# Scores of a token with itself and with its block-of-two neighbour: products by element, summed with a matrix of ones

## The chip, the core and the metric

The kernel runs on one core of a Trainium2 chip. A core has a matrix engine (PE, TensorE), a vector engine (DVE, VectorE), a scalar engine (ACT, ScalarE), GpSimd (POOL) and a queue engine (SP) that issues DMAs. Each engine works through its own list of instructions in order and waits on semaphores for the others. PE writes its results into PSUM; the other operands lie in SBUF, 128 partitions wide. The metric is device time in microseconds of one execution, lower being better; the median of three runs is given.

## The reference, cut to what matters

One encoder layer on 256 tokens of 2048 channels: a bidirectional HGRN2 mixer (gated linear recurrence, 16 heads of 128 channels, both directions summed), an output projection, a gated feed-forward net with a short convolution, RMS norms around each. The part that the change touches is the recurrence, which the kernel computes as a matrix of scores per head:

```python
def step(S, inp):
    qi, ki, gi, vi = inp
    b = jnp.cumsum(gi, axis=2)
    inter = jnp.einsum('nhtk,nhkv->nhtv', qi * jnp.exp(b), S)
    diff = b[:, :, :, None, :] - b[:, :, None, :, :]
    decay = jnp.exp(jnp.where(causal_in_chunk, diff, -jnp.inf))
    scores = jnp.einsum('nhtk,nhsk,nhtsk->nhts', qi, ki, decay)
    intra = jnp.einsum('nhts,nhsv->nhtv', scores, vi)
    ...
```

With forget gates f (one set for each direction) and k = 1 - f, the score of token t with an earlier token s is the sum over the 128 channels of q(t) k(s) times all gates from s+1 to t; the backward direction mirrors it. A token's score with itself is the sum of q(t) (k_forward(t) + k_backward(t)).

## The kernel before, in words

**Matrix products.** All weights are fp32. For each `sub` (256 rows by 512 columns of a weight matrix) ACT rounds the raw tile to fp32r (`whi`, L129) and DVE takes the remainder (`wlo = raw - whi`, L130). The activations are split the same way, and PE multiplies hi by hi, hi by lo and lo by hi. `gemm` (L140, matmuls at L174, L177 and L178, 12 of 512 columns per sub) gives tokens on partitions; `gemm_t` (L185, L206 with 512 columns and L209 with 256, 8 of each per sub) gives channels on partitions. `prep` runs LOOK = 3 subs ahead of PE, and `whi` and `wlo` have 4 buffers each, so ACT may write a buffer once PE has finished with the sub four places earlier.

**Scores.** The 16 heads are handled in four groups of HG = 4. For a group, q, the gates f and k = 1 - f of both directions lie with channels on partitions: `qT`, `f`, `ks` and `qs` (tiles of 128 x 1024 per direction; `qs` is q times the gate). The scores of a head with 256 tokens are two 128 x 128 diagonal blocks (`Sd`, eight per group) and two blocks across the halves (`So`). `Sd` is put together by doubling. `diag` (L407) adds the two directions of k into `kc` (L410), multiplies kc and q on PE (L415, eight fp32 matmuls of 128 columns in two calls) and keeps the diagonal with a product by the identity (L416). `level(lev)` (L426) for lev = 0 to 6 fills the pairs whose tokens lie in the two halves of a block of 2m tokens, m = 2^lev: eight fp32 matmuls of 128 columns (L435) of `kc` with `halves(qs, m)`, which takes each block's first m columns from one direction and its other m from the other direction, 1024 + m elements away; then `ks` and `qs` are multiplied by gates for the next level (L439, L442), the gates by each other (`bp`, L446), and the scores are copied into `Sd` where a mask says so (L454). `gather` (L422, on ACT) copies the same interleaving of `ks` into `kc`, which has one buffer. `across` (L456) makes `So`.

**What sets the order.** These closures are put into the queue `later` (two diag, seven levels, two across), and `gemm` and `gemm_t` take one closure from `soon` or `later` after each sub (`step`, L102), so the scores' work is strewn among the next projections' matmuls. The build then lists the instructions of each engine in an order of its own, by a simulated timeline, so that the order on an engine isn't that of the code. The score matmuls use PSUM tiles with the tag `tp`, which has two buffers. `nat` is a pool whose tags have two buffers (`qn` holds gate and sigmoid intermediates); tags of `hp` have one unless it says otherwise (`kc`, `bp0`).

Of the kernel before, what the change touches and what calls it, by code (L numbers as in the profile page):

```python
# [11 lines left out]
F32 = mybir.dt.float32  # L12
F32R = mybir.dt.float32r
U8 = mybir.dt.uint8
AF = mybir.ActivationFunctionType
ALU = mybir.AluOpType
AX = mybir.AxisListType

P = 128
T = 256  # L20
# [3 lines left out]
HG = 4  # L24
# [22 lines left out]
def encoder_layer(  # L47
# [12 lines left out]
    nc = tc.nc  # L60
    V, S, G = nc.vector, nc.scalar, nc.gpsimd

    def pool(stack, name, bufs=1, **kw):
        return stack.enter_context(tc.tile_pool(name=name, bufs=bufs, **kw))
# [14 lines left out]
    ident = const.tile([P, P], F32, name="ident")  # L79
# [20 lines left out]
    soon, later, extra = deque(), deque(), []  # L100
# [229 lines left out]
    rstack = ExitStack()  # L330
    hp = pool(rstack, "hgrn")
    nat = pool(rstack, "nat", 2)
    nsub_h = 2 * HG

    def silu_nat(ps, m, dst):
# [48 lines left out]
    def cut(t, off, dims):  # L384
        return bass.AP(t.tensor, t.offset + off, [list(t.ap[0])] + dims)

    def halves(t, m, c0=0, n=HG * T):


        return cut(t, c0, [[2 * m, n // (2 * m)], [HG * T + m, 2], [1, m]])  # L390

    def do_scores(g):

        q, ks, qs = st["q", g], st["k", g], st["d", g]  # L400
        Sd = hp.tile([P, nsub_h, P], F32, name="Sd", tag="Sd", bufs=2)
        So = [hp.tile([P, HG, P], F32, name="So", tag=f"So{d}", bufs=2) for d in range(2)]
        st["S", g] = (Sd, So)
        bp = [st["f", g]]
        kc = [None]

        def diag(i):  # L407
            if i == 0:
                kc[0] = hp.tile([P, HG, T], F32, name="kc", tag="kc")
                V.tensor_tensor(kc[0], ks[:, 0], ks[:, 1], op=ALU.add)  # L410
            sc = ps_t.tile([P, HG, P], F32, name="sc", tag="tp")
            for j in range(HG):
                h, b = (HG * i + j) // 2, (HG * i + j) % 2
                sl = slice(b * P, (b + 1) * P)
                nc.tensor.matmul(sc[:, j, :], kc[0][:, h, sl], q[:, h, sl], start=True, stop=True)  # L415
            V.tensor_tensor(  # L416
                Sd[:, HG * i : HG * i + HG, :], sc, ident[:, None, :].broadcast_to([P, HG, P]), op=ALU.mult
            )
            if i == 1:
                gather(1)  # L420

        def gather(m):  # L422
            kc[0] = hp.tile([P, HG, T], F32, name="kc", tag="kc")
            S.copy(kc[0].rearrange("p h (n two m) -> p (h n) two m", two=2, m=m), halves(ks, m))  # L424

        def level(lev):  # L426
            m = 1 << lev
            scs = []
            for i in range(2):
                sc = ps_t.tile([P, HG, P], F32, name="sc", tag="tp")  # L430
                for j in range(HG):
                    h, b = (HG * i + j) // 2, (HG * i + j) % 2
                    sl = slice(b * P, (b + 1) * P)
                    r = halves(qs, m, h * T + b * P, P)
                    nc.tensor.matmul(sc[:, j, :], kc[0][:, h, sl], r, start=True, stop=True)  # L435
                scs.append(sc)
            w = HG * T // m
            act = lambda t: cut(t, 0, [[HG * T + m, 2], [2 * m, w // 2], [1, m]])
            V.tensor_tensor(act(ks), act(ks), cut(bp[0], 1, [[w - 1, 2], [2, w // 2], [0, m]]), op=ALU.mult)  # L439
            if lev < NLEV - 1:  # L440
                gather(2 * m)
            V.tensor_tensor(act(qs), act(qs), cut(bp[0], w + 1, [[-(w + 1), 2], [2, w // 2], [0, m]]), op=ALU.mult)  # L442
            if lev < NLEV - 1:
                nbp = hp.tile([P, 2, w // 2], F32, name="bp", tag=f"bp{lev}")
                bv = cut(bp[0], 0, [[2, w], [1, 2]])
                V.tensor_tensor(nbp.rearrange("p d n -> p (d n)"), bv[:, :, 0], bv[:, :, 1], op=ALU.mult)  # L446
                bp[0] = nbp
            for i, sc in enumerate(scs):
                sd = Sd[:, HG * i : HG * i + HG, :]
                if lev == NLEV - 1:  # L450
                    S.copy(sd[:m, :, m:], sc[:m, :, m:])
                    S.copy(sd[m:, :, :m], sc[m:, :, :m])
                else:
                    V.copy_predicated(sd, mk[:, lev, None, :].broadcast_to([P, HG, P]), sc)  # L454

        def across(d):  # L456
            sc = ps_t.tile([P, HG, P], F32, name="sc", tag="tp")
            s0, t0 = d * P, (1 - d) * P
            for h in range(HG):
                nc.tensor.matmul(  # L460
                    sc[:, h, :], ks[:, d, h, s0 : s0 + P], qs[:, 1 - d, h, t0 : t0 + P], start=True, stop=True
                )
            S.copy(So[d], sc)

        later.extend([lambda: diag(0), lambda: diag(1)])
        later.extend([lambda lev=lev: level(lev) for lev in range(NLEV)])
        later.extend([lambda: across(0), lambda: across(1)])

# [48 lines left out]
    for part, g in ORDER:  # L517
        if part == "q":
            do_q(g)
        elif part == "f":  # L520
            do_f(g, 0)
        elif part == "b":
            do_f(g, 1)
            do_scores(g)
        elif part == "g":
            do_g(g)
        else:
            do_v(g)
            do_o(g)
# [221 lines left out]
```

## Time and profile before

| what | value |
|---|---|
| median of 3 runs | 1376.47 us (1376.24 to 1377.78) |
| the profiled execution, its own time | 1377.04 us |
| its span (first to last instruction) | 1375.3 us |
| granted TensorE clock, mean | 0.998 |
| ACT busy | 695.0 us (51%) |
| POOL busy | 13.5 us (1%) |
| HBM traffic | 248.93 MB, mean 181 GB/s |

Busy time of an engine is the time in which at least one of its instructions runs. PE's matmuls overlap in the profile: a row's mean duration covers the pipeline, and the rate has to be taken from how far apart their starts lie. A 128-column fp32 matmul of the program appears as two PE instructions (eight of them as x16). The times in the views of the trace count from the span's start. The scores of the four groups are made from about 90 to 157, 222 to 289, 355 to 422 and 461 to 552 us.

### The profile page before, as it was taken

The page shows a single profiled execution, that of the slowest core. Times are in us where ns is not written, and L with a number is a line of the kernel's source. Part 1 is how long each engine was busy: PE and PEld are TensorE (multiplying, and loading weights), DVE is VectorE, ACT ScalarE, POOL GpSimd, SP SyncE. Part 2 cuts the span into 40 slices and gives each one's busy share as a digit, 9 for nine tenths or more (in the row PEclk, how much of TensorE's full clock was granted, in tenths as well). Part 3 has the DMA queues.
Part 4 walks back from the last instruction along what each step waited for, and adds up shares of the span by engine and source line. Part 5 has one row for each costly group of instructions (what it writes and reads, how often), then busy time and mean ns, then how long its engine had stood idle before and what let it go on. Part 6 is the DMA issues. An engine that isn't in the chain of part 4 may idle for free.

```text
span 1375.3 us, 18411 instructions
## 1 busy us (share of the span) xinstructions
PE 1364.0 (99%) x7362; PEld 1180.4 (86%) x7362; DVE 940.1 (68%) x1188; ACT 695.0 (51%) x971; POOL 13.5 (1%) x21
## 2 busy tenths in 40 slices
PE   9999999999999999999999999999999999999997
PEld 7888988898898888888888888888888888888886
DVE  5687678866886876567668676877677775444444
ACT  5644454454544444456655555555555554434442
POOL 0000000000000000000000000000000000000000
PEclk9999999999999999999999999999999999999999
DMA  7554355435535444663555555555555555555552
GB/s 282 185 187 150 124 186 181 153 124 186 181 123 184 157 149 153 245 235 109 207 184 183 197 181 203 184 184 185 186 198 183 197 184 214 193 204 183 191 205 94
DMA packets 36998, 248.93 MB, mean 181 GB/s; under 512 B 4144, under 2 KB 4912, under 8 KB 7472
## 3 DMA queue, kind: packets, MB, share of 16 engines
q1 hardware_dynamic: 36912, 247.75, 51.2%
q8 instruction: 58, 0.95, 0.3%
q14 instruction: 28, 0.23, 0.0%
HBM read 245.63 MB, written 2.10 MB: 180 GB/s over the span
## 4 chain that ended last, share of the span: by engine, by line
PE 98%; issue 0%; DMA 0%; DVE 0%; SPq 0%; ACT 0%; DVEq 0%; POOLq 0%; POOL 0%
PE pg L206 36%; PE pg L209 18%; PE pg L178 13%; PE pg L177 13%; PE pg L174 13%; PE sc L435 4%; PE sc L491 1%; PE sc L460 1%; PE sc L492 1%; PE sc L415 1%; DMA xs<-in_x 0%; PE tp L233 0%; PE tp L587 0%; PE tp L290 0%; DVE fw L688 0%
## 5 line engine op out<-in xcount | busy, mean ns | idle before, releaser
L130 DVE TENSOR_TENSOR wlo<-raw,whi 128x1024 fp32r<-128x1024 f32 (+1 forms) x457 | 556.6, 1220 | 364.8 <-ACT whi L129 364.4
L129 ACT CAST whi<-raw 128x1024 fp32r<-128x1024 f32 (+1 forms) x457 | 478.3, 1049 | 508.8 <-PE pg L178 226.1
L206 PE MATMUL pg<-hh,whi 128*128 128x512 f32 x1344 | 355.2, 393 | 0.0
L206 PEld LDWEIGHTS pg<-hh,whi 128*128 128x128 f32 x1344 | 234.1, 189 | 34.7
L209 PEld LDWEIGHTS pg<-hh,wlo 128*128 128x128 f32 x1344 | 197.4, 190 | 22.6
L206 PE MATMUL pg<-xx,whi 128*128 128x512 f32 x768 | 208.6, 399 | 0.1
L209 PE MATMUL pg<-hh,wlo 128*128 128x256 f32 x1344 | 203.3, 281 | 0.0
L206 PEld LDWEIGHTS pg<-xx,whi 128*128 128x128 f32 x768 | 134.6, 190 | 20.2 <-DVE xx L298 0.7
L174 PE MATMUL pg<-whi,gg 128*128 128x512 f32 x352 | 136.9, 389 | 0.0
L177 PE MATMUL pg<-wlo,gg 128*128 128x512 f32 x352 | 136.9, 389 | 0.0
L178 PE MATMUL pg<-whi,gg 128*128 128x512 f32 x352 | 136.9, 389 | 0.0
L209 PEld LDWEIGHTS pg<-xx,wlo 128*128 128x128 f32 x768 | 113.0, 191 | 12.4
L209 PE MATMUL pg<-xx,wlo 128*128 128x256 f32 x768 | 117.4, 283 | 0.0
L177 PE MATMUL pg<-wlo,xx 128*128 128x512 f32 x256 | 101.0, 395 | 0.0
L174 PE MATMUL pg<-whi,xx 128*128 128x512 f32 x256 | 100.2, 391 | 0.0
L178 PE MATMUL pg<-whi,xx 128*128 128x512 f32 x256 | 100.0, 390 | 0.0
L177 PEld LDWEIGHTS pg<-wlo,gg 128*128 128x128 f32 x352 | 66.1, 188 | 13.8
L174 PEld LDWEIGHTS pg<-whi,gg 128*128 128x128 f32 x352 | 66.1, 188 | 13.7
L178 PEld LDWEIGHTS pg<-whi,gg 128*128 128x128 f32 x352 | 66.1, 188 | 13.5
L435 PEld LDWEIGHTS sc<-qs,kc 128*128 128x128 f32 x448 | 57.6, 192 | 1.9
L424 ACT COPY kc<-ks 128x1024 f32<-128x1024 f32 x28 | 32.1, 1147 | 52.4 <-PE sc L435 48.5
L435 PE MATMUL sc<-qs,kc 128*128 128x128 f32 x448 | 58.5, 285 | 0.0
(128 smaller groups left out, 1187.3 us busy)
## 6 DMA issues: line engine op xcount, KB each, us to landing
raw<-in_w_up SPq DMA_DIRECT2D x88, 1024.0 KB, 4.9
raw<-in_w_in SPq DMA_DIRECT2D x78, 1024.0 KB, 4.9
raw<-in_w_dn SPq DMA_DIRECT2D x44, 1024.0 KB, 4.9
raw<-in_w_o SPq DMA_DIRECT2D x16, 1024.0 KB, 4.9
x<-in_x SPq DMA_DIRECT2D x1, 2048.0 KB, 7.9
wp<-in_post SPq DMA_DIRECT2D x2, 1024.0 KB, 5.7
out<-fw SPq DMA_DIRECT2D x8, 256.0 KB, 2.6
xs<-in_x SPq DMA_DIRECT2D x3, 512.0 KB, 9.9
```

The source lines that it names most:

```text
L129: S.copy(hi[:, j], src[:, j])
L130: V.tensor_tensor(lo[:, j], src[:, j], hi[:, j].bitcast(F32), op=ALU.subtract)
L174: mm = nc.tensor.matmul(ps[m], a, hi[:, j, :], start=(k == 0), stop=False)
L177: nc.tensor.matmul(ps[m], a, lo[:, j, :], start=False, stop=False)
L178: nc.tensor.matmul(ps[m], b, hi[:, j, :], start=False, stop=(k == 2 * nsub - 1))
L206: nc.tensor.matmul(ps[n], w, xx[:, k], start=(k == 0), stop=False)
L209: nc.tensor.matmul(ps[n][:, 0, :], w, xx[:, k, 0, :], start=False, stop=(k == 2 * nsub - 1))
L415: nc.tensor.matmul(sc[:, j, :], kc[0][:, h, sl], q[:, h, sl], start=True, stop=True)
L424: S.copy(kc[0].rearrange("p h (n two m) -> p (h n) two m", two=2, m=m), halves(ks, m))
L435: nc.tensor.matmul(sc[:, j, :], kc[0][:, h, sl], r, start=True, stop=True)
L460: nc.tensor.matmul(sc[:, h, :], ks[:, d, h, s0 : s0 + P], qs[:, 1 - d, h, t0 : t0 + P], start=True, stop=True)
L491: nc.tensor.matmul(o[:, h, :], Sd[:, 2 * h + b, :], v[:, b, cs], start=True, stop=False)
```

## The change

The self scores and the level-0 scores aren't taken from a full 128 x 128 product any more. The two operands are multiplied element by element on DVE (`products`, a tile `pr` of 128 x 1024), the product is split into an fp32r part `prh` (ACT) and a remainder `prl` (DVE), and PE sums both over the channels by a matmul with a 128 x 128 matrix of ones as weights and 512 columns moving (`sums`). Each row of the result holds the sums of all tokens, of which the identity (self) or the mask of level 0 picks its own. `own` makes the products for the self scores; `diag` sums them, makes the products for level 0 and writes the diagonal; level 0 sums instead of multiplying. The gather into `kc` for level 0 is gone; `prh` lives in the buffer of `kc`, `prl` in that of `bp0`, `pr` in `qn`. The closures in `later` are as many as before.

```diff
+    ones = hp.tile([P, P], F32R, name="ones")
+    S.activation(ones, ident, AF.Copy, scale=0.0, bias=1.0)
...
-        def diag(i):
-            if i == 0:
-                kc[0] = hp.tile([P, HG, T], F32, name="kc", tag="kc")
-                V.tensor_tensor(kc[0], ks[:, 0], ks[:, 1], op=ALU.add)
+        def products(k, r, p=None):
+            if p is None:
+                p = nat.tile([P, HG * T], F32, name="pr", tag="qn")
+            V.tensor_tensor(p.rearrange("p (n j) -> p n j", j=2), k, r, op=ALU.mult)
+            ph = hp.tile([P, HG * T], F32R, name="prh", tag="kc")
+            pl = hp.tile([P, HG * T], F32R, name="prl", tag="bp0")
+            S.copy(ph, p)
+            V.tensor_tensor(pl, p, ph.bitcast(F32), op=ALU.subtract)
+            pr[0] = (ph, pl)
+
+        def sums(i):
             sc = ps_t.tile([P, HG, P], F32, name="sc", tag="tp")
-            for j in range(HG):
-                h, b = (HG * i + j) // 2, (HG * i + j) % 2
-                sl = slice(b * P, (b + 1) * P)
-                nc.tensor.matmul(sc[:, j, :], kc[0][:, h, sl], q[:, h, sl], start=True, stop=True)
-            V.tensor_tensor(
-                Sd[:, HG * i : HG * i + HG, :], sc, ident[:, None, :].broadcast_to([P, HG, P]), op=ALU.mult
-            )
-            if i == 1:
-                gather(1)
+            o = sc.rearrange("p h t -> p (h t)")
+            for j, a in enumerate(pr[0]):
+                nc.tensor.matmul(o, ones, a[:, i * 512 : i * 512 + 512], start=(j == 0), stop=(j == 1))
+            return sc
+
+        def own():
+            p = nat.tile([P, HG * T], F32, name="pr", tag="qn")
+            V.tensor_tensor(p.rearrange("p (h t) -> p h t", t=T), ks[:, 0], ks[:, 1], op=ALU.add)
+            pairs = lambda t: t.rearrange("p (n j) -> p n j", j=2)
+            products(pairs(p), pairs(q.rearrange("p h t -> p (h t)")), p)
+
+        def diag():
+            scs = [sums(i) for i in range(2)]
+            w = HG * T
+            products(cut(ks, w + 1, [[2, w // 2], [-(w + 1), 2]]), cut(qs, 0, [[2, w // 2], [w + 1, 2]]))
+            for i, sc in enumerate(scs):
+                V.tensor_tensor(
+                    Sd[:, HG * i : HG * i + HG, :], sc, ident[:, None, :].broadcast_to([P, HG, P]), op=ALU.mult
+                )
...
             for i in range(2):
+                if lev == 0:
+                    scs.append(sums(i))
+                    continue
                 sc = ps_t.tile([P, HG, P], F32, name="sc", tag="tp")
...
-        later.extend([lambda: diag(0), lambda: diag(1)])
+        later.extend([own, diag])
```

The lines behind the insertions move: in the changed kernel the sum of the two directions is L433, the products L417, the remainder L421, the sums L428, the updates of `ks`, `qs` and `bp` L466, L469 and L473, the diagonal L442, the masked copies L481 and the level matmuls L462.

On DVE, in the first group, from the point where the second direction's `ks` and `qs` are done, the kernel before has:

```order
L446 TENSOR_TENSOR bp<-f 128x1024
L410 TENSOR_TENSOR kc<-ks 128x1024
L130 TENSOR_TENSOR wlo<-raw,whi 128x1024
L446 TENSOR_TENSOR bp<-bp 128x512
L130 TENSOR_TENSOR wlo<-raw,whi 128x1024
L446 TENSOR_TENSOR bp<-bp 128x256
L130 TENSOR_TENSOR wlo<-raw,whi 128x1024
L446 TENSOR_TENSOR bp<-bp 128x128
L446 TENSOR_TENSOR bp<-bp 128x64
L446 TENSOR_TENSOR bp<-bp 128x32
L416 TENSOR_TENSOR Sd<-sc,ident 128x512
```

The changed kernel has at the same place:

```order
L433 TENSOR_TENSOR pr<-ks 128x1024
L130 TENSOR_TENSOR wlo<-raw,whi 128x1024
L417 TENSOR_TENSOR pr<-ks,qs 128x1024
L417 TENSOR_TENSOR pr<-pr,qT 128x1024
L130 TENSOR_TENSOR wlo<-raw,whi 128x1024
L466 TENSOR_TENSOR ks<-ks,f 128x2x512
L469 TENSOR_TENSOR qs<-qs,f 128x2x512
L130 TENSOR_TENSOR wlo<-raw,whi 128x1024
L421 TENSOR_TENSOR prl<-pr,prh 128x1024
L130 TENSOR_TENSOR wlo<-raw,whi 128x1024 x2
L340 SCALAR_TENSOR_TENSOR gg<-pg,rs_137,sg 128x512 x2
L130 TENSOR_TENSOR wlo<-raw,whi 128x1024
```

Both products and the level-0 updates of `ks` and `qs` now stand ahead of the diagonal, with `wlo` operations between them, and the products of gates (`bp`) come after level 0 (its first stands behind the first masked copy).

On PE, the kernel before has the first group's self scores in one piece between the matmuls of a projection:

```order
L177 MATMUL pg<-wlo,xx 128x512
L178 MATMUL pg<-whi,xx 128x512
L174 MATMUL pg<-whi,xx 128x512
L415 MATMUL sc<-qT,kc 128x128 x8
L177 MATMUL pg<-wlo,xx 128x512
```

The changed kernel has, for the level-0 sums of the same group:

```order
L428 MATMUL sc<-prh,ones 128x512
L174 MATMUL pg<-whi,xx 128x512
L177 MATMUL pg<-wlo,xx 128x512
L178 MATMUL pg<-whi,xx 128x512
L174 MATMUL pg<-whi,xx 128x512
L428 MATMUL sc<-prl,ones 128x512
L177 MATMUL pg<-wlo,xx 128x512
L178 MATMUL pg<-whi,xx 128x512
L428 MATMUL sc<-prh,ones 128x512
L428 MATMUL sc<-prl,ones 128x512
```

The sums stand singly among the projection's matmuls. Counting the projections' 512-column matmuls that stand ahead of them in PE's list, the first score matmul of group 0 moves from behind 265 to behind 281, its first level-0 matmul from behind 289 to behind 324, and its level-1 matmuls from behind 320 to behind 353. The remainders of the self scores (`prl`, L428) stand behind 300, the first of level 0 behind 328. In the third group (`ks` and `qs` of which are needed while the fourth group's q and f are projected) `across` moves from behind 680 of the 256-column matmuls to behind 704, the last of that projection.

More of the change, by code (lines that the diff above doesn't have):

```diff
@@ L405, in do_scores @@
         kc = [None]
-        def diag(i):
-            if i == 0:
-                kc[0] = hp.tile([P, HG, T], F32, name="kc", tag="kc")
-                V.tensor_tensor(kc[0], ks[:, 0], ks[:, 1], op=ALU.add)
-            sc = ps_t.tile([P, HG, P], F32, name="sc", tag="tp")
-            for j in range(HG):
-                h, b = (HG * i + j) // 2, (HG * i + j) % 2
-                sl = slice(b * P, (b + 1) * P)
-                nc.tensor.matmul(sc[:, j, :], kc[0][:, h, sl], q[:, h, sl], start=True, stop=True)
-            V.tensor_tensor(
-                Sd[:, HG * i : HG * i + HG, :], sc, ident[:, None, :].broadcast_to([P, HG, P]), op=ALU.mult
-            )
-            if i == 1:
-                gather(1)
+        pr = [None]
+        def products(k, r, p=None):
[8 more added lines that the diff above has]
+        def sums(i):
+            sc = ps_t.tile([P, HG, P], F32, name="sc", tag="tp")
+            o = sc.rearrange("p h t -> p (h t)")
[15 more added lines that the diff above has]
+                )
         def gather(m):
```

## The prediction

> **What bounds the kernel now.** I read the page first: the span, the busy shares and the chain that ended last.
>
> ```profile
> span 1375.3 us, 18411 instructions
> PE 1364.0 (99%) x7362; PEld 1180.4 (86%) x7362; DVE 940.1 (68%) x1188; ACT 695.0 (51%) x971; POOL 13.5 (1%) x21
> PE 98%; issue 0%; DMA 0%; DVE 0%; SPq 0%; ACT 0%; DVEq 0%; POOLq 0%; POOL 0%
> PE pg L206 36%; PE pg L209 18%; PE pg L178 13%; PE pg L177 13%; PE pg L174 13%; PE sc L435 4%; PE sc L491 1%; PE sc L460 1%; PE sc L492 1%; PE sc L415 1%; DMA xs<-in_x 0%; PE tp L233 0%; PE tp L587 0%; PE tp L290 0%; DVE fw L688 0%
> ```
>
> The chain that sets the end is 98% PE, and the two lines that the change rewrites, L415 and L435, lie on it. A busy PE alone would prove little, since matmuls overlap, so the view of waits is asked for PE, and then for what the weights' preparation waits for.
>
> ```profile
> PE tp L290 <- DMA xs<-in_x: 1.6, 1, 1.6
> PE tp L269 <- POOL ident masks.py:199: 1.4, 1, 1.4
> ```
>
> ```profile
> DVE wlo L130 <- ACT whi L129: 364.4, 329, 3.4
> ACT whi L129 <- PE pg L178: 226.1, 148, 2.6
> ACT whi L129 <- PE pg L206: 209.5, 143, 3.1
> ```
>
> PE waits for data twice, both at the start, 3.0 us in all; it never waits for a weight or a score operand. Behind it the order of dependence is the reverse of starvation: DVE waits for ACT, and ACT waits for PE to give a buffer back. So a microsecond less on PE in the scores is a microsecond less of the span, as long as PE's operands still come in time.
>
> **What PE loses and gains.** The chain in order of time has each score step as one piece, start and duration:
>
> ```profile
> 98.69 1.78 PE sc L415 x16
> 105.93 2.66 PE sc L435 x16
> 115.64 1.92 PE sc L435 x16
> 123.25 1.78 PE sc L435 x16
> ...
> 469.11 1.78 PE sc L415 x16
> 476.35 2.66 PE sc L435 x16
> ```
>
> The self scores of a group cost 1.78 us, level 0 costs 2.66, level 1 costs 1.92 and the later ones 1.78. The first and the last of the four groups have the same durations (the two between them as well). The change removes 4 x (1.78 + 2.66) = 17.76 us from PE.
>
> It adds, per group, 2 steps x 2 halves x 2 parts = 8 fp32r matmuls of 512 columns, 32 in all. Their price is the distance from one to the next in a stretch that holds nothing but such matmuls, the last projection:
>
> ```profile
> 1135.00:1355.00 220.00, 220.00 (x973) 182.21 (x972) 105.92 (x93) 90.28 (x94) 0.00 (x0) 1.00 0.55 191
> ```
>
> The columns are the stretch, its length, then busy time and count of PE, weight loads, DVE, ACT and POOL, the granted clock, DMA share and rate. 220.00 / 973 = 0.226 us, at a granted clock of 1.00. No operation of before has a matrix of ones as its weights, but each of these 973 loads other weights too and all of that fits into the 0.226. So 32 x 0.226 = 7.23 us come back, and PE saves 17.76 - 7.23 = **10.5 us**. From above, the price is bounded by L206 in pieces of eight (1.84 us, 0.230 each, which gives 7.36); I see no reason for one cheaper than 0.226.
>
> **What DVE and ACT get, and what hides it.**
>
> ```profile
> L439 DVE TENSOR_TENSOR ks<-ks,f 128x1024 f32<-128x1024 f32 x4 | 4.9, 1226 | 0.2
> L410 DVE TENSOR_TENSOR kc<-ks 128x1024 f32<-128x1024 f32 x4 | 4.9, 1218 | 0.0
> L130 DVE TENSOR_TENSOR wlo<-raw,whi 128x1024 fp32r<-128x1024 f32 x455 | 555.2, 1223 | 362.2 <-ACT whi L129 361.8
> L129 ACT CAST whi<-raw 128x1024 fp32r<-128x1024 f32 x455 | 477.0, 1051 | 505.5 <-PE pg L178 226.1 <-PE pg L206 209.5 <-issue 56.6
> ```
>
> Rows that give the operation, busy us and mean ns. The sum of the two k (L410) stays. New on DVE per group are two products and two remainders, on ACT two casts. A remainder has L130's shape, 1.22 us, and a cast L129's, 1.05. The self product is contiguous, 1.22 us like L410. The neighbour product is new to the trace: both of its operands jump 1025 elements back or forth at every element. Its lower bound is 1.22, that of L439's first level, which steps over every second element. For an upper bound there are the jumps that ACT makes in the gathers:
>
> ```profile
> 100.52 1.55 ACT L424 COPY kc<-ks 128x1024 f32<-128x1024 f32 x1 [0.96 <-PE sc L415]
> 108.63 1.21 ACT L424 COPY kc<-ks 128x1024 f32<-128x1024 f32 x1 [1.26 <-PE sc L435]
> 117.60 1.06 ACT L424 COPY kc<-ks 128x1024 f32<-128x1024 f32 x1 [2.68 <-PE sc L435]
> ```
>
> Jumping at each element costs ACT 1.55 against 1.06, a factor of 1.5, the same that PE pays at level 0 (2.66 against 1.78). With that factor the product takes 1.8 us. I take 1.8, since the pattern is the same, and keep 1.2 to 1.8: DVE gets 3 x 1.22 + 1.8 = 5.5 us more per group (4.9 to 5.5). ACT gets 2 x 1.05 - 1.55 = 0.55 us, which is nothing beside 1375.3 - 695.0 = 680 us of idle time.
>
> [...] The three gathers and the three level durations above agree: one element per visit is slow, two (level 1) cost 1.92 against 1.78, four nothing. [...]
>
> Is there room on DVE? The windows of the four groups' score stages, columns as above:
>
> ```profile
> 90.00:157.00 67.00, 67.00 (x377) 58.81 (x376) 55.13 (x58) 31.58 (x35) 0.00 (x0) 1.00 0.45 157
> 222.00:289.00 67.00, 67.00 (x376) 58.78 (x375) 55.37 (x59) 31.49 (x34) 0.00 (x0) 1.00 0.45 157
> 355.00:422.00 67.00, 67.00 (x411) 60.08 (x411) 57.57 (x64) 32.43 (x38) 0.00 (x0) 1.00 0.44 153
> 461.00:552.00 91.00, 91.00 (x491) 78.83 (x490) 66.00 (x77) 44.76 (x63) 2.01 (x2) 1.00 0.43 150
> ```
>
> DVE idles 11.9, 11.6, 9.4 and 25.0 us in them. The stages get 2.6 us shorter, so 9.3, 9.0, 6.8 and 22.4 remain for 5.5 us. It fits, in the third group by 1.3 us only. The second test is local: the first group's densest stretch, DVE and ACT in order of time (start, duration).
>
> ```profile
> 91.64 1.22 DVE L446 TENSOR_TENSOR bp<-f 128x1024 f32<-128x1024 f32 x1
> 92.78 1.22 DVE L410 TENSOR_TENSOR kc<-ks 128x1024 f32<-128x1024 f32 x1
> ...
> 97.12 1.22 DVE L130 TENSOR_TENSOR wlo<-raw,whi 128x1024 fp32r<-128x1024 f32 x1
> ```
>
> ```profile
> 95.78 1.06 ACT L129 CAST whi<-raw 128x1024 fp32r<-128x1024 f32 x1 [1.61 <-PE pg L178]
> ...
> 98.50 1.05 ACT L129 CAST whi<-raw 128x1024 fp32r<-128x1024 f32 x1 [1.66 <-PE pg L178]
> ```
>
> ACT casts as soon as PE frees a buffer, three subs (36 x 0.226 = 8.1 us) before PE needs the result. The weights cast at 95.78 are needed at 103.9; their remainder is done at 98.3, 5.6 us early. By the changed order the new sum stands where `bp` stood at 91.64, and ahead of this third remainder come a remainder, two products, a remainder and two updates. At 1.14 us from start to start (92.78 - 91.64), and 0.6 more for the slow product, it starts at 91.64 + 7 x 1.14 + 0.6 = 100.2 and is done at 101.4: still 2.5 us early. The next, behind `prl`, starts at 102.5 and is done at 103.7; it is needed at 98.50 + 8.1 = 106.6, so 2.9 early.
>
> The sums themselves are new waits for PE. Both parts wait for `pr` (DVE), `prh` (ACT) and `prl` (DVE). By its place PE reaches the first sum 16 matmuls after 98.69, at 102.3, and the first remainder 19 matmuls and two sums later, at 107.0; `prl` is done at 102.6. Behind the diagonal of the self scores (from about 107.6, 0.7 us) comes the remainder of level 0, done near 109.6; PE reads it at 107.0 + 0.45 + 28 x 0.226 + 0.23 = 114.0. So each has some 4 us in hand, as L410 had before (done 94.0, used at 98.69). What the cover is worth if it goes: PE holds up everything queued behind a sum, projections included, microsecond by microsecond.
>
> `prl` shares `bp0`'s buffer, so the first product of gates now waits for level 0's sums; it was early work before and is needed only by level 1's update of `ks`. The last group's scores reach the output projection 23 matmuls (5.2 us) later, and in the third group `across` moves behind the fourth group's f; DVE's writes of `f` wait for it, and the weights behind them. I cost both at nothing: PE fills such stretches with other subs, and needs those gates only a projection (8 subs, 22 us) later. Matrix of ones: one small ACT operation at the start, while ACT waits for the first DMA.
>
> **The sum.** The profiled execution took 1377.04 us, 0.57 above the median of 1376.47, so 1377.04 - 10.5 = 1366.5 (from the median, 1365.9). A measurement of this kernel tells a change of about 0.2%, 2.75 us, from none.
>
> **Rivals.** *PE waits for the sums or for weights here and there.* Eight first uses (two steps, four groups), each late by up to one DVE operation, 1.22 us; for it: products, cast and remainder are a chain over three engines, and the third group has only 1.3 us to spare. Against it: 2.5 to 4.5 us in hand in the first. At half of it 8 x 0.61 = 4.9 us are given back: 1371.4. In full, 9.8 come back: 1376.3, no change, which is also the case in which the change doesn't do what it says.
>
> *The sums are dearer than a projection's matmul.* If each took the 0.393 us that the groups give as the mean of such a matmul (a latency, overlapping the next), 32 x 0.393 = 12.6, and the saving is 5.2: 1371.8. The 973 matmuls in 220 us speak against it.
>
> *DVE becomes the bound: slower.* DVE's idle time lies where it waits for PE's scores or ACT's casts. If the new operations can't move into it because each waits behind a score copy, and the weights' remainders behind them, then 5.5 us per group come onto the path: 1366.5 + 22 = 1388.5. It decides when the remainders lose more than 2.5 us of their lead, that is when the neighbour product takes over 4.3 us or DVE stands over 2.5 us at one diagonal; nothing in the trace comes near the first.
>
> **How the numbers follow.** Forecast 0.79; waits of some microseconds 0.10; dear sums 0.03; all given back 0.05; DVE the bound 0.03. Faster by over 0.2%: 0.79 + 0.10 + 0.03 = 0.92; the same 0.05; slower 0.03. The forecast's own range is 1364.8 to 1368: runs of before differ by 1.5 us, the price of a sum by 0.13. For 8 in 10 the range reaches into the waits' case: 1364.8 to 1370.5, which leaves out the 0.11 of the last three and somewhat less than half of the first rival's 0.10. Dear sums lie just outside.
>
> **What would show it.** In the chain, L428 pieces of about 0.23 us and no L415; level matmuls from 1.92 us down; no 2.66. PE's waits still only the two at the start: any wait of a sum or of L174, L177, L206 or L209 is the first rival. The neighbour product's row says 1.2 or 1.8. DVE about 960 us busy, PE near 1353. Wrong: PE idle time in 90 to 550 us, or sums spaced wider than 0.23.

## The result, and the profile after

| | before | after |
|---|---|---|
| median of five runs each | 1376.59 us (1376.24 to 1377.78) | 1365.39 us (1364.97 to 1366.09) |
| the profiled execution, its own time | 1377.04 us | 1365.48 us |
| its span | 1375.3 us | 1363.7 us |
| granted TensorE clock, mean | 0.998 | 0.998 |

The changed kernel is faster by 11.2 us: ratio 0.9918, interval 0.9907 to 0.9928. The page of the changed kernel, with span, busy times, and the chain that ended last by engine and by line:

```profile
span 1363.7 us, 18236 instructions
PE 1351.4 (99%) x7266; PEld 1167.3 (86%) x7266; DVE 955.5 (70%) x1204; ACT 698.0 (51%) x976; POOL 13.5 (1%) x21
PE 98%; DMA 1%; issue 0%; SPq 0%; DVE 0%; ACT 0%; DVEq 0%; POOLq 0%; POOL 0%
PE pg L206 35%; PE pg L209 18%; PE pg L174 13%; PE pg L178 13%; PE pg L177 13%; PE sc L462 3%; DMA raw<-in_w_in 1%; PE sc L428 1%; PE sc L519 1%; PE sc L487 1%; PE sc L518 1%; PE tp L233 0%; PE tp L614 0%; SPq L115 0%; DVE fw L715 0%
```

The chain is still 98% PE: no other engine has moved onto it. What PE waits for in the changed kernel (us in total, times, longest), and what the weights' remainders wait for:

```profile
PE tp L290 <- DMA xs<-in_x: 2.5, 1, 2.5
PE tp L269 <- POOL ident masks.py:199: 1.4, 1, 1.4
PE pg L206 <- DVE xx L298: 0.3, 1, 0.3
```

```profile
DVE wlo L130 <- ACT whi L129: 334.4, 309, 3.2
```

All three waits of PE lie at the start, ahead of everything that was changed; no sum, no level and no weight is among them. The chain in order of time, first group (start, duration):

```profile
101.75 0.45 PE sc L428 x2
106.51 0.45 PE sc L428 x2
112.40 0.23 PE sc L428
113.54 0.23 PE sc L428
114.22 0.45 PE sc L428 x2
119.88 1.92 PE sc L462 x16
```

The pieces of 1.78 and 2.66 us are gone; in their place are twice four sums of 0.23, and the levels begin with 1.92. To see where the time was gained, one matmul of the program is looked up in both chains: an L206 ahead of the scores, and the first L206 behind all four groups. Before:

```profile
45.36 1.84 PE pg L206 x8
...
656.75 1.81 PE pg L206 x8
```

After:

```profile
44.79 1.84 PE pg L206 x8
...
645.21 1.81 PE pg L206 x8
```

Of the 11.6 us of span, 45.36 - 44.79 = 0.57 is there before the changed part begins. In the other kernels below, the same matmul starts between 44.1 and 45.7, so this is scatter of the start. The stretch between the two went from 611.39 to 600.42 us: 10.97 us, 2.74 for a group. What follows compares this stretch, or the medians.

### The profile page after: what moved, and what is told of

Read it like the earlier page. It is cut to its first block, busy times and chain, and to the rows that moved or that the text cites. A ratio compares the mean times of both kernels' runs of the same rounds, so it can differ in the third digit from the quotient of the medians.

```text
span 1363.7 us, 18236 instructions
## 1 busy us (share of the span) xinstructions
PE 1351.4 (99%) x7266; PEld 1167.3 (86%) x7266; DVE 955.5 (70%) x1204; ACT 698.0 (51%) x976; POOL 13.5 (1%) x21
## 4 chain that ended last, share of the span: by engine, by line
PE 98%; DMA 1%; issue 0%; SPq 0%; DVE 0%; ACT 0%; DVEq 0%; POOLq 0%; POOL 0%
PE pg L206 35%; PE pg L209 18%; PE pg L174 13%; PE pg L178 13%; PE pg L177 13%; PE sc L462 3%; DMA raw<-in_w_in 1%; PE sc L428 1%; PE sc L519 1%; PE sc L487 1%; PE sc L518 1%; PE tp L233 0%; PE tp L614 0%; SPq L115 0%; DVE fw L715 0%
## 5 line engine op out<-in xcount | busy, mean ns | idle before, releaser
L206 PE MATMUL pg<-hh,whi 128*128 128x512 f32 x1344 | 355.2, 393 | 0.0
L206 PEld LDWEIGHTS pg<-hh,whi 128*128 128x128 f32 x1344 | 234.1, 189 | 34.7
L206 PE MATMUL pg<-xx,whi 128*128 128x512 f32 x768 | 206.4, 397 | 0.3 <-DVE xx L298 0.3
L206 PEld LDWEIGHTS pg<-xx,whi 128*128 128x128 f32 x768 | 134.8, 190 | 20.7 <-DVE xx L298 0.5
L174 PEld LDWEIGHTS pg<-whi,gg 128*128 128x128 f32 x352 | 66.1, 188 | 13.6
L178 PEld LDWEIGHTS pg<-whi,xx 128*128 128x128 f32 x256 | 48.1, 188 | 9.7
L177 PEld LDWEIGHTS pg<-wlo,xx 128*128 128x128 f32 x256 | 48.1, 188 | 9.8
L174 PEld LDWEIGHTS pg<-whi,xx 128*128 128x128 f32 x256 | 48.1, 188 | 9.7
```

The costliest lines, as they stand in the source:

```text
L174: mm = nc.tensor.matmul(ps[m], a, hi[:, j, :], start=(k == 0), stop=False)
L177: nc.tensor.matmul(ps[m], a, lo[:, j, :], start=False, stop=False)
L178: nc.tensor.matmul(ps[m], b, hi[:, j, :], start=False, stop=(k == 2 * nsub - 1))
L206: nc.tensor.matmul(ps[n], w, xx[:, k], start=(k == 0), stop=False)
```

## Experiments

Each ratio is to runs of the kernel before on the same chip, whose medians were 1376.4 to 1376.8 us.

**Each half of the change alone.** The first kernel has the self scores by sums and level 0 as before; the second has the self scores as before and level 0 by sums.

```diff
 def diag():
     scs = [sums(i) for i in range(2)]
-    products(cut(ks, w + 1, [[2, w // 2], [-(w + 1), 2]]), cut(qs, 0, [[2, w // 2], [w + 1, 2]]))
...
+    gather(1)
 def level(lev):
-        if lev == 0:
-            scs.append(sums(i))
-            continue
```

```diff
-def own():
...
-def diag():
+def diag(i):
+    if i == 0:
+        kc[0] = hp.tile([P, HG, T], F32, name="kc", tag="kc")
+        V.tensor_tensor(kc[0], ks[:, 0], ks[:, 1], op=ALU.add)
...
+        nc.tensor.matmul(sc[:, j, :], kc[0][:, h, sl], q[:, h, sl], start=True, stop=True)
...
+    if i == 1:
+        products(cut(ks, w + 1, [[2, w // 2], [-(w + 1), 2]]), cut(qs, 0, [[2, w // 2], [w + 1, 2]]))
```

> Only the self scores are taken by products and ones; level 0 is as in the kernel before. Theory (PE time alone counts): four groups save 1.78 - 4 x 0.227 = 0.87 us each, 3.5 us: 1373.1. Rival (the gain lies in the new order of instructions and hangs on no single step): about half of the 11.2 us, 1371.

> Only level 0 is taken by products and ones; the self scores are as in the kernel before. Theory: four groups save 2.66 - 0.91 = 1.75 us each, 7.0 us: 1369.6. Rival (order): 1371. The two single parts together should save what the change saves, 11.2 us.

Self scores alone: 1372.56 us, ratio 0.9969 (0.9956 to 0.9981). Level 0 alone: 1369.21 us, 0.9945 (0.9931 to 0.9958). Both lie near what PE's time alone gives (1373.1 and 1369.6), not at the 1371 of the rival by which the new order is what saves. Between the same two matmuls they gain 3.7 and 7.2 us. That is 10.9 together, against 10.97 for the change: the halves add up, and neither makes the other wait. The chain of the first kernel still has the long level 0, that of the second the old self scores:

```profile
107.00 2.66 PE sc L458 x16
```

```profile
96.96 1.78 PE sc L439 x16
```

**Sums in fp32, without the split.** One fp32 matmul with the unrounded products takes the place of two fp32r matmuls; the cast and the remainder go.

```diff
-    ones = hp.tile([P, P], F32R, name="ones")
+    ones = hp.tile([P, P], F32, name="ones")
...
-    ph = hp.tile([P, HG * T], F32R, name="prh", tag="kc")
-    pl = hp.tile([P, HG * T], F32R, name="prl", tag="bp0")
-    S.copy(ph, p)
-    V.tensor_tensor(pl, p, ph.bitcast(F32), op=ALU.subtract)
-    pr[0] = (ph, pl)
+    pr[0] = (p,)
```

> The products aren't split: ones and products are fp32, four sums of 512 columns per group where the change has eight; ACT's two casts and DVE's two remainders per group are gone. Theory (PE is paid by columns times passes): an fp32 matmul of 512 columns takes four times one of 128 (0.222), 0.89 us, so a step costs 1.78 us, and of the change only the strided surplus of level 0 is left, 4 x 0.88 = 3.5 us: 1373.1. Rival (fewer, wider instructions and fewer weight loads are what saves): as fast as the change or faster, 1365.4 or below.

1371.98 us, 0.9966 (0.9953 to 0.9978). The chain shows the price of the step:

```profile
103.53 1.72 PE sc L424 x4
```

Two fp32 matmuls (four PE instructions) take 1.72 us, where four fp32r sums take 0.91. A group's two steps then cost 3.44 us instead of the 4.44 of before: 4 x 1.00 = 4.0 us of gain, which is what the stretch between the two matmuls shows (4.0). So the products alone bring 4.0 us, and the split into fp32r parts brings the other 7. Less work for DVE and ACT bought nothing.

**Without the remainders.** Only the rounded products are summed; the sums lose `prl`.

```diff
-    pl = hp.tile([P, HG * T], F32R, name="prl", tag="bp0")
...
-    V.tensor_tensor(pl, p, ph.bitcast(F32), op=ALU.subtract)
-    pr[0] = (ph, pl)
+    pr[0] = (ph,)
```

> Leaves out the remainders: only the rounded products are summed. 16 matmuls fewer on PE, 16 x 0.227 = 3.6 us: 1361.8. Eight remainders fewer on DVE, 9.8 us of its time: if DVE's added work costs anything in the changed kernel, the gain is larger than 3.6; by the theory it isn't.

1361.97 us, 0.9891 (0.9877 to 0.9904), 3.4 us below the change. Sixteen sums at 0.226 are 3.6. Eight DVE operations fewer add nothing to it. This is the fastest kernel of the study; whether its sums are precise enough for a use of the kernel is another question.

**How much free time has DVE?** An addition over 128 x 1024, whose result nobody reads, is put at the start of levels: one in levels 1, 3 and 5 (N is 0 in the others), one in each, and two in each. A group then has 3, 7 or 14 more of them, of 1.22 us each.

```diff
 def level(lev):
+    for _ in range(N):
+        jd = hp.tile([P, HG, T], mybir.dt.bfloat16, name="jd", tag="jd")
+        V.tensor_tensor(jd, ks[:, 0], ks[:, 1], op=ALU.add)
```

> The changed kernel with three more DVE operations of 128 x 1024 per group, at levels 1, 3 and 5, whose result nobody reads: 3 x 1.22 x 4 = 14.6 us more on DVE. Theory (DVE has 8.3, 8.3, 5.2 and 19.9 us free in the four stages): 1365.4, no change. Rival (DVE's work comes onto the path): 1380.

> The same with one such operation at each of the seven levels, 8.5 us per group. Theory: groups 0 and 1 are just full, group 2 is over by 3.3 us, so between 1365.4 and 1369.4. Rival: 1399.

> The same with two at each level, 17.1 us per group. Theory: over the free time by 8.8, 8.8 and 11.9 us in groups 0 to 2 and not in group 3, about 29.5 us: 1395, with PE waiting for weights. Below 1375: work moves out of the stages into idle time around them. Rival (all on the path): 1434.

Three more: 1365.28 us, 0.9919 (0.9905 to 0.9933). Seven more: 1365.80, 0.9921 (0.9908 to 0.9935). Neither can be told from the change. Fourteen more: 1373.69 us, 0.9979 (0.9970 to 0.9988), 8.3 above it. The window of the third group's sums and first levels with seven more (the stretch, its length, busy time and count of PE, weight loads, DVE, ACT and POOL, granted clock, DMA share and rate), and the fourteen's row of additions:

```profile
349.70:416.70 67.00, 67.00 (x390) 59.08 (x389) 65.11 (x72) 33.90 (x39) 0.00 (x0) 1.00 0.46 158
```

```profile
L454 DVE TENSOR_TENSOR jd<-ks 128x1024 bf16<-128x1024 f32 x56 | 68.1, 1217 | 0.0
```

DVE is 97% busy there (65.11 of 67.00 us), PE is busy for the whole stretch, and the time is that of the change. But the build lists the instructions anew for each of these kernels: here the third group's `across` starts at 435.4 us on PE, in the change at 420.4, so a part of what was added lies behind this window. With fourteen, 68.1 us of DVE work are added and 8.3 come onto the path. That is below 1375, where the expectation has the work move out of the stages into idle time around them, and far from the 1395 of its theory. PE's waits in that kernel, beside the start's:

```profile
PE tp L233 <- DVE og L532: 3.1, 2, 2.0
...
PE pg L174 <- ACT oo L539: 0.8, 1, 0.8
...
PE sc L465 <- DVE oo L540: 0.6, 1, 0.6
```

`oo` and `og` are results of whole groups: 0.8 and 0.6 us are waited where the third group's outputs are handed on (both between 530 and 540 us, amid the last group's scores), 3.1 where the last group's outputs are transposed for the output projection. No weight and no operand of a score is waited for. Two windows from that place, the first transpose (start, duration, and the idle time before it), and a matmul behind the transposes in the chain:

```profile
564.83:568.24 3.41, 1.45 (x14) 1.26 (x13) 1.57 (x7) 1.96 (x15) 1.01 (x1) 1.00 0.62 202
568.24:575.07 6.83, 5.69 (x16) 4.18 (x17) 2.63 (x6) 1.37 (x2) 1.01 (x1) 0.50 1.00 363
```

```profile
568.22 0.47 PE L233 MATMUL tp<-ident,og 128*128 128x128 f32 x1 [1.96 <-DVE og L532]
```

```profile
572.30 0.43 PE pg L177
```

PE was busy for 1.45 of 3.41 us at the full clock, and from 568.2 to 575.1 the granted clock is 0.50. The first transpose starts at the moment of the fall and takes 0.47 us, where the changed kernel's takes 0.27; the other transposes and the projection run at half speed as well (0.43 us a matmul instead of 0.226). By that ratio about 2.7 of the 5.69 us that PE is busy there are due to the clock, which is an estimate. So the 8.3 us are 1.4 of waiting at the third group's outputs, 3.1 at the last group's and some 2.7 of slow clock; about 1.1 us are not accounted for. Ahead of the fall from 1.00 to 0.50 stands an idle piece of 1.96 us, with PE busy for 1.45 of the 3.41 us that ended with the fall. The other 1.1 us of waiting came when the clock was already at half.

**Which groups make the last one late?** Fourteen additions per group, in the first three groups only (below), and in the last one only (`g == NG - 1` in the same place).

```diff
-    for _ in range(2):
+    for _ in range(2 if g < NG - 1 else 0):
```

> The load of dve_14 (two extra DVE operations at each level, 17.1 us per group) in the first three groups only. New theory (VectorE's lateness costs only where the last group's scores meet the output projection and PE has nothing else to do): 1365.4, no change. Rival (the weights' remainders come late wherever DVE is full): three quarters of the 8.3 us, 1371.6.

> The same load in the last group only. New theory: all of the 8.3 us, 1373.7, with PE waiting for the transposes of og (about 3 us) and a granted clock below 1 in the stretch after it. Rival: one quarter, 1367.5.

1366.89 us, 0.9932 (0.9920 to 0.9945), and 1366.76 us, 0.9929 (0.9916 to 0.9943): each costs about 1.4 us. The new theory expected 1365.4 and 1373.7, the rival 1371.6 and 1367.5: neither fits both. The time at which the last group's `across` begins on PE (timeline: start, duration), in the change, with the first three groups loaded, with the last one loaded, and with all:

```profile
542.48 1.95 PE L487 MATMUL sc<-qs,ks 128*128 128x128 f32 x16
```

```profile
550.64 1.95 PE L490 MATMUL sc<-qs,ks 128*128 128x128 f32 x16
```

```profile
550.77 1.95 PE L490 MATMUL sc<-qs,ks 128*128 128x128 f32 x16
```

```profile
558.00 1.95 PE L490 MATMUL sc<-qs,ks 128*128 128x128 f32 x16
```

The lateness adds up: 8.2 and 8.3 us alone, 15.5 together; so it is carried from the first groups into the last. It is carried by the order of the program. The matmuls of the projections (tile `pg`) that PE has run until then, first in the change, then with all groups loaded:

```profile
0.00:542.48 542.48, 475.23 (x2376) 393.96 (x2376) 25.43 (x56) 28.36 (x64) 1.00 0.49 173
```

```profile
0.00:558.00 558.00, 489.04 (x2436) 404.87 (x2436) 24.99 (x56) 28.09 (x64) 1.00 0.49 172
```

With either load alone the same window counts 2412. PE works in the order of its list, and with one load it waits for nothing between the start and 566 us: the 36 matmuls more (36 x 0.226 = 8.1 us) stand ahead of `across` in the list that the build made for the loaded kernel. With both loads 60 more make 13.6 us, and the waits of 1.4 us come on top. So these runs load DVE and move the scores at once; what the same load does to the order of the change was not run.

The cost doesn't add up: 1.4 and 1.4, but 8.3 together. Ahead of the transposes of the last group PE has run 2448 such matmuls in each of the three loaded kernels, so 36 of them (8.1 us) cover the way from `across` to the transposes with one load, as in the change (2376 to 2412), and only 12 (2.7 us) with both. With one of the two loads, the window at that place reads:

```profile
565.00:570.00 5.00, 4.15 (x20) 3.28 (x18) 2.55 (x3) 1.60 (x3) 0.00 (x0) 1.00 0.97 392
```

PE idles 0.85 us and the clock stays at 1.00. With both it idles 1.96 us, the clock falls, and it idles 1.1 us more.

**How much of the gain is the strided operand?** In the kernel before, level 0 takes its moving operand from one direction, contiguous, instead of alternating between two; the scores of level 0 are then those of one direction.

```diff
-    r = halves(qs, m, h * T + b * P, P)
+    r = halves(qs, m, h * T + b * P, P) if lev else qs[:, 0, h, sl]
```

> The kernel before, with level 0's moving operand replaced by contiguous columns of one direction (the pairing of tokens is left out, so level 0's scores are other ones). Theory (the surplus of level 0 is the jump at each element): its pieces take 1.78 instead of 2.66 us, 4 x 0.88 = 3.5 us less than before: 1373.1. Rival (the surplus is that of the first use of kc, or of a wait): 1376.6.

1373.41 us, 0.9975 (0.9966 to 0.9984). The piece goes from 2.66 to 1.78 us:

```profile
106.31 1.78 PE sc L435 x16
```

4 x 0.88 = 3.5 us, and 3.5 between the two matmuls. So a third of what the change gains is the surplus of that operand's jumps; the rest is that 128-column fp32 products are replaced.

**What does the jump cost DVE?** The neighbour product with one jumping operand instead of two; the k of each pair then comes from one direction.

```diff
-    cut(ks, w + 1, [[2, w // 2], [-(w + 1), 2]])
+    cut(ks, 0, [[2, w // 2], [1, 2]])
```

> The neighbour product's k operand is read in contiguous order and only its q operand jumps at each element (the pairing is left out, so level 0's scores are other ones). The time stays at 1365.4 by every theory, since the product is hidden. Its row says 1.50 us if one jumping operand sets the pace, 1.36 if each adds its share, 1.22 if it takes two.

1365.67 us, 0.9921 (0.9903 to 0.9939), no difference to the change. Its product's row:

```profile
L417 DVE TENSOR_TENSOR pr<-ks,qs 128x1024 f32<-128x1024 f32 x4 | 6.0, 1488 | 0.0
```

One jumping operand sets the pace: 1.49 us, with two 1.50.

## Why the prediction was right, point by point

The forecast of 1366.5 for the profiled execution came out at 1365.48, 0.57 of the difference being the start's scatter.

**PE loses 17.76 us and gets 7.23 back: right, 0.5 us too small.** The term of 10.5 measured 11.0 in the stretch between the two matmuls. Each half has its share: 3.7 instead of 3.5, and 7.2 instead of 7.0. The price of a sum as one reads it in the chain is the forecast's (0.45 for two), and not the 0.39 of the rival with dear sums, which is the mean duration of a matmul that overlaps the next:

```profile
L428 PEld LDWEIGHTS sc<-prh,ones 128*128 128x128 f32 x16 | 3.0, 188 | 0.6
L428 PE MATMUL sc<-prh,ones 128*128 128x512 f32 x16 | 5.6, 389 | 0.0
```

Between the two matmuls, taking 16 sums away brought 3.48 us, 0.218 each. The kernel with fp32 sums takes 6.96 us longer than the change for 8 x 1.72 = 13.76 us of such sums, which leaves 6.80 us for the 32, 0.212 each. Both are a little below the 0.226 of the row; 0.014 less for each of 32 sums would account for most of the 0.5 us. No row shows where a sum runs faster, so this stays open. PE's busy time came out at 1351.4 instead of 1353, for the same reason and because PE waited 4.2 us at the start instead of 3.0.

**DVE gets 5.5 us a group: the neighbour product was put too high.**

```profile
L417 DVE TENSOR_TENSOR pr<-ks,qs 128x1024 f32<-128x1024 f32 x4 | 6.0, 1502 | 0.0
L417 DVE TENSOR_TENSOR pr<-pr,qT 128x1024 f32<-128x1024 f32 x4 | 4.9, 1220 | 0.0
L421 DVE TENSOR_TENSOR prl<-pr,prh 128x1024 fp32r<-128x1024 f32 x8 | 9.7, 1218 | 0.0
L420 ACT CAST prh<-pr 128x1024 fp32r<-128x1024 f32 x8 | 8.4, 1047 | 1.9 <-PE sc L428 1.9
```

It takes 1.50 us, between the bounds of 1.2 and 1.8 and nearly halfway. I had carried PE's and ACT's factor of 1.5 over to DVE; DVE's is 1.502 / 1.220 = 1.23. The jump costs DVE time as well, but less than it costs PE (2.66 / 1.78 = 1.49) and ACT (1.55 / 1.06 = 1.46). Two elements in succession weren't quite full speed either (1.92 against 1.78 us on PE, 1.21 against 1.06 on ACT). The other three rows are as costed. DVE's busy time rose by 15.4 us, not by 20: busy time counts overlapping instructions once, and the new ones start 1.14 us apart where they last 1.22. The remainder of this difference stays open.

**What hides it: confirmed.** Windows as long as those of before, shifted with the work:

```profile
90.00:157.00 67.00, 67.00 (x370) 58.27 (x369) 58.70 (x63) 33.49 (x36) 0.00 (x0) 1.00 0.47 164
219.37:286.37 67.00, 67.00 (x370) 58.26 (x369) 58.67 (x63) 33.48 (x36) 0.00 (x0) 1.00 0.47 164
349.74:416.74 67.00, 67.00 (x401) 59.48 (x400) 61.80 (x68) 33.75 (x40) 0.00 (x0) 1.00 0.46 161
453.10:544.10 91.00, 91.00 (x478) 78.02 (x477) 71.13 (x82) 45.37 (x64) 2.01 (x2) 1.00 0.46 162
```

DVE still idles 8.3, 8.3, 5.2 and 19.9 us. That is more than the 3.8, 3.5, 1.3 and 16.9 that the prediction leaves, but the two aren't the same stretch: the prediction's is 2.6 us shorter, and the first three windows here end about 4 us before the groups' `across` (161.2, 290.7 and 420.4 us). The local test held too. DVE and ACT in the first group's densest stretch:

```profile
99.30 1.23 DVE L130 TENSOR_TENSOR wlo<-raw,whi 128x1024 fp32r<-128x1024 f32 x1
100.43 1.23 DVE L421 TENSOR_TENSOR prl<-pr,prh 128x1024 fp32r<-128x1024 f32 x1
...
107.69 1.22 DVE L421 TENSOR_TENSOR prl<-pr,prh 128x1024 fp32r<-128x1024 f32 x1
```

```profile
95.21 1.05 ACT L129 CAST whi<-raw 128x1024 fp32r<-128x1024 f32 x1 [1.61 <-PE pg L178]
```

The third remainder is done at 100.5 and needed at 95.21 + 8.1 = 103.3: 2.8 us early, where 2.5 was predicted. The first `prl` is done at 101.7 and read at 106.4, the second at 108.9 and 113.4: over 4 us in hand, as said. PE came to the first sum, the first remainder and that of level 0 at 101.8, 106.5 and 113.5, where 102.3, 107.0 and 114.0 were worked out; the start's 0.57 is the difference.

**The first rival (PE waits)** has nothing for it: no wait beyond the start, and the two halves add up.

**The slower rival had the wrong place and the wrong point.** It was to decide when the weights' remainders lose more than 2.5 us of their lead. By the prediction's count the third group had 1.3 us to spare, so that three additions (3.7 us) would have been too many. Seven (8.5 us a group) did nothing, and even with fourteen no weight was waited for, in both with the scores listed later than in the change. The first thing to be late is what I had costed at nothing, "the last group's scores reach the output projection 23 matmuls later". The end of that group in the changed kernel, DVE and PE:

```profile
554.35 1.13 DVE L529 SCALAR_TENSOR_TENSOR og<-sc,ro,gg 128x128 f32<-128x128 f32 x4 [1.19 <-POOL ro L215]
```

```profile
556.03 0.27 PE L233 MATMUL tp<-ident,og 128*128 128x128 f32 x1
```

The outputs are done at 555.5, and PE transposes them from 556.0; most (seven of the eight) from 556.6, 1.1 us later. Nothing was lost in the changed kernel. But at this point PE can run out of other work (busy for 1.45 of 3.41 us with fourteen additions), and so a later end of the scores comes onto the path here, at first for little, and with the clock's fall for much.

## What to carry to other kernels

When PE sets the end, replace a small fp32 product of which only a diagonal is used by a product by element and a sum over a matrix of ones, but split the products into two fp32r parts: without the split, less than half of the gain was left. Price what PE loses and gains from the distance between starts, and look at the hidden work by a load test: add operations to the hiding engine until the time moves, and see where it does. Where a build orders the instructions itself, compare the orders too: here the loaded kernels had the scores later in PE's list. The first place to cost time was where the last stage hands its result to the next, not the densest stretch, and there, with fourteen additions per group, the granted clock fell from 1.00 to 0.50, so that by the estimate above some 2.7 us of slow work came on top of 3.1 us of waiting.

## What the runs showed of the hardware

- An operand that jumped between two regions at each element cost PE a factor of 2.66 / 1.78 = 1.49, ACT 1.55 / 1.06 = 1.46 and DVE 1.502 / 1.220 = 1.23, and on DVE one such operand was about as slow as two (1.488 against 1.502 us).
- With either load of fourteen alone, 0.85 us of PE idle in 5.00 us left the granted clock at 1.00. With all four groups loaded, an idle piece of 1.96 us, in 3.41 us of which PE was busy for 1.45, ended with the clock at 0.50, which is the mean of the 6.83 us that follow.
- The ones were loaded as weights again for each sum (32 loads of 0.188 us in the rows of L428); the loads lay beside the matmuls, and two sums took 0.45 us in the chain, no more than two matmuls of a projection at 0.226.
